# A 31-tap depthwise convolution: 28 instead of 25 taps of each second chunk on TensorE, as three products of split operands, with the diagonals built by GpSimd

## Chip, core and metric

The kernel runs on one core of a Trainium2 chip. The metric is the device time of one execution in microseconds (us). Engines are named as in the profile: PE is TensorE (PEld its weight loads), DVE VectorE, ACT ScalarE, POOL GpSimd, SP SyncE, which here only issues DMAs.

## What is computed

A stack of two blocks over 256 tokens of width 1024, all in float32. The change is in one layer of the second block, a convolution module between a feed-forward layer and a cross attention:

```python
def conformer_conv(x, norm, w1, b1, dw_w, dw_b, ln_g, ln_b, w2, b2):
    h = rms_norm_2(x, norm) @ w1 + b1
    h = jax.nn.glu(h, axis=-1)
    h = causal_dwconv(h, dw_w, dw_b)
    h = jax.nn.silu(layer_norm_2(h, ln_g, ln_b))
    return h @ w2 + b2
```

`causal_dwconv` has 31 taps: each of the 1024 features is summed over itself and its 30 predecessors in time, each with a weight of its own per feature. The rest of the stack (attention forms, recurrences, pooling, feed-forward layers) is the same in both kernels.

## The kernel before

Features stand on the 128 partitions and the 256 tokens along the free dimension, so the 1024 features of the convolution are eight chunks of 128 x 256. Every weight matrix comes from DRAM in pieces of 128x1024 (`raw`); ACT rounds a piece to `wh`, DVE subtracts to get the rest, `wl` (L289 and L290, the helper `weights`), and each product is three matmuls of 256 columns: high by high, high by low, low by high (L302, the helper `mm_F`, results `psF`).

The function `conformer` goes over four pairs of chunks. For a pair it projects the gate and the value (`psF`), scales both out of PSUM on DVE (`c_g` L1061, `c_a` L1064), applies tanh and bias on ACT, and forms the gated value `a` (the second `c_a`, L1069). Then it convolves. `CONV_PE = (0, 25) + (0, 25) * 3` says how many taps of a chunk go to TensorE: none of the first chunk of a pair, 25 of the second. The other taps are DVE instructions that add one shifted, weighted copy to `c_h` (L1094, SCALAR_TENSOR_TENSOR): 30 for the first chunk after one TENSOR_SCALAR (L1087), 6 for the second. A tap on TensorE is a matmul of `a` with a diagonal matrix of that tap's weights, in plain float32, accumulated in one bank, `ps_conv`; the diagonals `c_diag` are 100 ACT instructions (L1081, identity times a column of weights). ACT then moves `ps_conv` with the bias to `c_h` (L1085).

After the last pair a filler follows, two projections of the next layer's memory (`kF`, whose products are `psF` too), and then the layer norm over features: `c_acc` (L1099, L1101) sums the chunks on DVE, `ps_mean` (L1104) sums partitions on PE.

A scheduler orders the instructions of each engine before the run; on the chip each engine works through its list in that order, and an instruction that waits holds up those behind it. Tiles of one tag share a fixed number of buffers: tag `f4` has 9, used in this layer by `c_h` (two tiles, the second from the third pair on) and by `c_diag`; a new tile waits until the readers of an old one are done. On POOL the kernel before has only small work: the power in the reciprocal rms (`x_rc`, L111), masks, memsets. The `x_rc` of this layer stands right before the first pair.

Of the kernel before, what the change touches and what calls it, by code (L numbers as in the profile page):

```python
# [11 lines left out]
F32 = mybir.dt.float32  # L12
# [18 lines left out]
def shape_constants():  # L31
    """Tables that depend on shapes alone."""
    t = np.arange(S, dtype=np.float64)
    gamma = 1.0 - 2.0 ** (-5.0 - np.arange(NH, dtype=np.float64))
    dec = np.zeros((128, 3, NH, 128), np.float64)
    for b, (s0, t0) in enumerate(((0, 0), (0, 128), (128, 128))):
        s, q = t[s0:s0 + 128, None], t[None, t0:t0 + 128]
        seen = (s // CHUNK) <= (q // CHUNK)
        for h in range(NH):
            dec[:, b, h] = np.where(seen, gamma[h] ** np.abs(q - s), 0.0) * 128.0 ** -0.5  # L40
    misc = np.zeros((128, 32), np.float64)
    misc[:, 0] = 10000.0 ** (-(np.arange(128) % 64) / 64.0)
    misc[:, 1] = np.where(np.arange(128) < 64, 1.0, -1.0)
    misc[:, 16:32] = 1.0 / np.arange(1, 17)
    return dec.reshape(128, -1).astype(np.float32), misc.astype(np.float32)


CONV_PE = (0, 25) + (0, 25) * 3
KV_AHEAD = 400
# [4 lines left out]
def stack_kernel(ctx: ExitStack, tc: tile.TileContext, I: dict, out: bass.AP):  # L54
# [16 lines left out]
    def t_f4(shape, name):  # L71
        return f4.tile(shape, F32, tag="f4", name=name)
# [18 lines left out]
    def bc(ap, n):  # L91
        """[128, m] -> [128, n, m]"""
        return ap.unsqueeze(1).to_broadcast([ap.shape[0], n, ap.shape[1]])

    # ---------------------------------------------------------------- constants
    ident = const.tile([128, 128], F32, name="ident")
# [15 lines left out]

    # ---------------------------------------------------------------- activations in
    def load_T(src, name):
        """[256, 1024] -> four pairs [128 features, 2 chunks, 256 tokens]"""
        raws = []
        for t in range(2):
            raw = wraw.tile([128, D], F32, tag="wraw", name=name + "_raw")
            nc.sync.dma_start(raw, src[t * 128:(t + 1) * 128, :])
            raws.append(raw)  # L120
        return raws
# [3 lines left out]

    # ---------------------------------------------------------------- parameters as columns
    order = ["norm_pre", "norm_post", "mem_norm", "conv_q", "conv_k",
# [43 lines left out]

    # ---------------------------------------------------------------- helpers
    def sums_to_rstd(acc, name):
        """acc [128, 256]: partial sums of squares -> column [128, 2] of 1 / rms"""
        ps = bank([128, 2], "ps_ss")
        for t in range(2):
            PE.matmul(ps[:, t:t + 1], acc[:, t * 128:(t + 1) * 128], ones[:, 0:1], start=(t == 0),
                      stop=True, skip_group_check=True)
        rc = t_sm([128, 2], name + "_rc")
        V.tensor_scalar(rc, ps, 1.0 / D, EPS, op0=ALU.mult, op1=ALU.add)  # L180
        rsqrt(rc, rc)
        return rc

    def row_of(rc, name):
        """column [128, 2] -> [128, 256], the same on each partition"""
        pb = bank([128, S], "ps_rb")
# [7 lines left out]
    def softplus_neg_abs(dst, src):  # L194
        """log(1 + exp(-|src|)), small tiles: 2 atanh(e / (2 + e)) as a series"""
        sh = [128, int(np.prod(src.shape[1:]))]
# [15 lines left out]
    class Sq:  # L212
        """sum of squares of four pairs of chunks, by partition"""

# [23 lines left out]
    class Operand:  # L238
        """float32 [128, n, 256] as two float32r parts whose sum it is"""

# [15 lines left out]
    class Norm:  # L256
        """what a layer reads of x: x times the gain as an operand, and the reciprocal rms"""

# [18 lines left out]
    def weights(src, n_k):  # L277
        """[n_k * 128, n] of DRAM -> slices (hi, lo) by chunk"""
        parts = []
# [14 lines left out]
    def mm_F(pss, src, op, k0, n_k, first, last):  # L294
        """features on partitions: banks of two chunks from the columns of src"""
        w = weights(src, n_k)
# [9 lines left out]
    def mm_T(pss, src, op, k0, n_k, first, last, extra=None):  # L306
        """tokens on partitions: two banks of 128 tokens by 512 columns"""
        w = weights(src, n_k)
# [27 lines left out]
    def scaled_F(pss, rb, dst):  # L336
        """dst [128, 4, 256] = psum * rstd"""
        for i in range(2):
            V.tensor_tensor(dst[:, 2 * i:2 * i + 2], pss[i], bc(rb, 2), op=ALU.mult)
# [17 lines left out]
    def silu2_F(w, c0, op, rb, name, pss=None):  # L357
        """2 * silu(projection), features on partitions"""
        z = F_plain(w, c0, op, rb, name, pss=pss)
# [5 lines left out]
    def silu2_T(w, c0, op, rc, name):  # L365
        """2 * silu(projection) / rstd, tokens on partitions"""
        pss = proj_T(w, c0, op)
# [8 lines left out]
    def taps(dst, src, wname, j0, stride, n_tap, first):  # L376
        """dst = causal convolution of src [128, 256] along time, per-feature taps"""
        tap = lambda j: col(wname, j0 + j * stride)
# [11 lines left out]
    def blocks(kF, qF, fn):  # L390
        """products of keys (partitions) and queries, by block of 128 x 128"""
        for b, (s, t) in enumerate(BLK):
# [10 lines left out]
    def T_to_operand(y, scale):  # L403
        """[128 tokens, 2, 512] -> operand of 4 chunks"""
        o = Operand(4, yop, "y")
# [10 lines left out]

    # ---------------------------------------------------------------- memory
    def mem_stats(src):
# [23 lines left out]

    # ---------------------------------------------------------------- rotary tables
    cosF = const.tile([128, S], F32, name="cosF")
# [28 lines left out]

    # ================================================================ block 1
    def layer(l, nrm, early, kv, late, nxt):
# [7 lines left out]
        rb = row[0]  # L483
        # small parameters
        bif = t_sm([128, 2, 4], "bif")
# [19 lines left out]

        # ---- stick breaking
        def sb_branch():
# [56 lines left out]

        # ---- mLSTM
        def conv_silu2(c0, wname, name):
            """2 * silu(causal convolution of a projection), features on partitions"""
            x = F_plain(w, c0, op, rb, name + "_x")
# [8 lines left out]
        def ml_branch():  # L577
            # gates: tokens on partitions, then rows
            ps = t_sm([128, 2, 8], "gsum")
# [111 lines left out]

        # ---- retention
        def rt_branch():
# [50 lines left out]

        # ---- gated mixing over tokens
        def gm_branch():
# [51 lines left out]

        # ---- attention to the memory
        def xa_branch():  # L800
# [25 lines left out]

        # ---- gated merge
        merged = [t_f4([128, 2, 512], "merged")
# [46 lines left out]
    def softmax(pairs, sc):  # L875
        """softmax over keys of sum of q^T k, queries on partitions: [128, 2, 256]"""
        pl = bank([128, 2, S], "ps_lg")
# [26 lines left out]

    # ================================================================ block 2
    def kv_k(op, rb, w, c0):
# [44 lines left out]
    def mixer_ab(nrm, fill_1, fill_2, nxt):  # L951
# [6 lines left out]
        rb = row[0]  # L958
        # ---- gated linear recurrence
        wgx = t_f4([128, 8, 128], "a_gx")  # L960
# [4 lines left out]
        for g4 in range(2):  # L965
# [15 lines left out]
            th = t_f4([128, 4, S], "a_th")  # L981
            # q = 1 - exp(la) = -tanh(la / 2) (1 + exp(la)); the squared multiplier is q (2 - q)
            A.activation(th, la, AF.Tanh, scale=-0.5)
# [11 lines left out]
        for g4 in range(2):  # L995
# [5 lines left out]
            for i in range(2):  # L1001
                ya.put(slice(2 * i, 2 * i + 2), z[:, 2 * i:2 * i + 2])
        # ---- pooling over several windows
        pss = proj_F(w, 2 * D, op)
# [44 lines left out]
    def conformer(nrm, fill_1, fill_2, nxt):  # L1049
# [8 lines left out]
        for i in range(4):  # L1058
# [12 lines left out]
            for m in range(2):  # L1071
# [3 lines left out]
                if n_pe:  # L1075
                    ps = bank([128, S], "ps_conv")
                    for j0 in range(0, n_pe, 8):
                        n = min(8, n_pe - j0)
                        dg = t_f4([128, 8, 128], "c_diag")
                        for j in range(j0, j0 + n):  # L1080
                            A.activation(dg[:, j - j0], ident, AF.Copy,  # L1081
                                         scale=col("c_dw_w_2", (30 - j) * 8 + c))
                            PE.matmul(ps[:, j:], dg[:, j - j0], a[:, m, 0:S - j], start=(j == 0),  # L1083
                                      stop=(j == n_pe - 1))
                    A.activation(h, ps, AF.Identity, bias=col("c_dw_b_2", c))  # L1085
# [130 lines left out]
    class Last:  # L1216
        """x times the last gain, in place, and the sums of squares of x"""

# [20 lines left out]

    # ================================================================ program  # L1240
    nrm = Norm("norm_pre", 0)
# [99 lines left out]
```

## Time and profile before

| | |
|---|---|
| median of 3 runs | 1837.79 us (1835.53 to 1839.57) |
| span of the profiled execution | 1834.2 us |
| stretch of the four pairs | about 1394 to 1496 us of the span |

The span is the time from the first to the last instruction of the one profiled execution. It lies 3.6 us under the median of the timed runs; that difference holds what is around the span and the scatter between executions. All positions below are microseconds from the start of the span. Busy time of PE is modelled: matmuls overlap, so the pace of TensorE is read from starts, not from durations.

### The profile page before, as it was taken

What the parts mean: (1) busy time and instruction counts of PE and PEld (TensorE: products, weight loads), DVE (VectorE), ACT (ScalarE), POOL (GpSimd) and SP (SyncE); (2) the same over time, 40 slices, a digit from 0 to 9 for tenths busy, and PEclk for the clock granted to TensorE, in tenths of its full rate; (3) what the DMA queues carried; (4) which work ended last, traced back from release to release, by engine and by line L of the source; (5) the groups of instructions that cost most, each with busy time, mean ns of one, the idle gap of its engine ahead of it and who ended that gap; (6) DMA issues with size and microseconds to landing.
All of it is one profiled execution on the core that took longest, in us unless ns stands there. A gap on an engine that the chain in (4) does not pass through costs nothing.

```text
span 1834.2 us, 30422 instructions
## 1 busy us (share of the span) xinstructions
PE 1788.3 (97%) x12246; PEld 1665.9 (91%) x12246; DVE 1264.4 (69%) x1883; ACT 963.0 (53%) x1372; POOL 40.2 (2%) x52
## 2 busy tenths in 40 slices
PE   7999999999999999999999899999999989999998
PEld 7988988888999899888899798999999989899998
DVE  5796855666657877666667965576669985477665
ACT  4764345454555543555456854455447545455444
POOL 0100000000000000000000000000000000000000
PEclk9999999999999999999999999999999999999999
DMA  6456455666554655567655454455554344355552
GB/s 212 150 179 197 153 183 157 195 208 193 161 161 145 201 166 165 153 196 230 193 186 161 146 177 144 141 182 184 184 184 143 104 134 150 113 175 186 183 184 92
DMA packets 168002, 309.56 MB, mean 169 GB/s; under 512 B 12620, under 2 KB 25268, under 8 KB 167860
## 3 DMA queue, kind: packets, MB, share of 16 engines
q1 hardware_dynamic: 166480, 307.08, 53.8%
q8 instruction: 96, 1.57, 0.4%
q10 hardware_dynamic: 1380, 0.53, 0.1%
q14 instruction: 46, 0.38, 0.1%
HBM read 306.52 MB, written 1.05 MB: 168 GB/s over the span
## 4 chain that ended last, share of the span: by engine, by line
PE 75%; issue 15%; DVE 5%; ACT 3%; DMA 1%; POOL 0%; SPq 0%; POOLq 0%; ACTq 0%; DVEq 0%
PE psF L302 35%; PE psT L315 19%; PE psO L302 14%; DVE c_h L1094 2%; DVE wl L290 1%; PE ps_conv L1083 1%; PE ps_lg L880 1%; PE ps_blk L395 1%; ACT wh L289 1%; PE ps_xo L1162 1%; DMA gm_wr<-in_gm_ws 1%; PE ps_rb L188 0%; PE ps_rt L724 0%; PE ps_num L650 0%; DMA raw<-in_w_in 0%
## 5 line engine op out<-in xcount | busy, mean ns | idle before, releaser
L290 DVE TENSOR_TENSOR wl<-raw,wh 128x1024 fp32r<-128x1024 f32 x560 | 670.6, 1222 | 337.7 <-ACT wh L289 330.3
L289 ACT ACTIVATE wh<-raw 128x1024 fp32r<-128x1024 f32 x560 | 574.9, 1055 | 515.8 <-PE psF L302 174.2
L302 PE MATMUL psF<-xh,wh 128*128 128x256 f32 x1888 | 539.6, 286 | 8.3 <-ACT wh L289 5.3
L302 PE MATMUL psF<-xh,wl 128*128 128x256 f32 x1888 | 536.2, 285 | 2.3 <-DVE wl L290 2.3
L302 PE MATMUL psF<-xl,wh 128*128 128x256 f32 x1888 | 536.7, 285 | 0.0
L302 PEld LDWEIGHTS psF<-xh,wh 128*128 128x128 f32 x1888 | 364.4, 193 | 10.2 <-ACT wh L289 6.1
L302 PEld LDWEIGHTS psF<-xh,wl 128*128 128x128 f32 x1888 | 364.0, 193 | 3.5 <-DVE wl L290 3.1
L302 PEld LDWEIGHTS psF<-xl,wh 128*128 128x128 f32 x1888 | 364.5, 193 | 0.6
L302 PE MATMUL psO<-yh,wh 128*128 128x256 f32 x800 | 225.7, 285 | 5.4 <-ACT yh L247 5.4
L302 PE MATMUL psO<-yl,wh 128*128 128x256 f32 x800 | 227.4, 285 | 0.5 <-DVE yl L248 0.5
L302 PE MATMUL psO<-yh,wl 128*128 128x256 f32 x800 | 226.1, 283 | 0.0
L315 PE MATMUL psT<-wh,xl 128*128 128x512 f32 x544 | 216.0, 397 | 0.0
L315 PE MATMUL psT<-wl,xh 128*128 128x512 f32 x544 | 215.4, 396 | 0.0
L315 PE MATMUL psT<-wh,xh 128*128 128x512 f32 x544 | 213.4, 392 | 0.0
L302 PEld LDWEIGHTS psO<-yh,wh 128*128 128x128 f32 x800 | 153.5, 193 | 6.4 <-ACT yh L247 6.4
L302 PEld LDWEIGHTS psO<-yl,wh 128*128 128x128 f32 x800 | 153.9, 193 | 0.9 <-DVE yl L248 0.7
L302 PEld LDWEIGHTS psO<-yh,wl 128*128 128x128 f32 x800 | 154.0, 193 | 0.1
L315 PEld LDWEIGHTS psT<-wl,xh 128*128 128x128 f32 x544 | 102.2, 188 | 21.0
L315 PEld LDWEIGHTS psT<-wh,xl 128*128 128x128 f32 x544 | 102.2, 188 | 20.6
L315 PEld LDWEIGHTS psT<-wh,xh 128*128 128x128 f32 x544 | 102.3, 188 | 19.2
L1094 DVE SCALAR_TENSOR_TENSOR c_h<-c_a,cols,c_h 128x229 f32<-128x229 f32 (+15 forms) x144 | 63.2, 464 | 3.0
L315 PE MATMUL psT<-wl,yh 128*128 128x512 f32 x160 | 62.3, 389 | 0.0
(379 smaller groups left out, 2115.4 us busy)
## 6 DMA issues: line engine op xcount, KB each, us to landing
raw<-in_w_in SPq DMA_DIRECT2D x224, 512.0 KB, 3.9
raw<-in_f_w_up SPq DMA_DIRECT2D x96, 512.0 KB, 4.7
raw<-in_f_w_down SPq DMA_DIRECT2D x48, 512.0 KB, 4.7
raw<-in_w_up SPq DMA_DIRECT2D x40, 512.0 KB, 3.5
raw<-in_c_w_pw SPq DMA_DIRECT2D x24, 512.0 KB, 4.4
raw<-in_ab_w_in SPq DMA_DIRECT2D x20, 512.0 KB, 3.7
raw<-in_w_mem_kv SPq DMA_DIRECT2D x16, 512.0 KB, 4.9
raw<-in_w_out SPq DMA_DIRECT2D x16, 512.0 KB, 3.8
```

Of the source, the lines that this page charges most:

```text
L289: A.activation(hi, raw, AF.Copy)
L290: V.tensor_tensor(lo, raw, hi.bitcast(F32), op=ALU.subtract)
L302: PE.matmul(pss[m // 2][:, m % 2], a, b, start=(first and m % 2 == 0 and k == 0 and n == 0), stop=(last and k == n_k - 1 and n == 2), skip ...
L315: PE.matmul(pss[t], a, b, start=(first and k == 0 and n == 0), stop=(last and k == n_k - 1 and n == 2), skip_group_check=True)
L395: PE.matmul(ps[:, h], kF[:, h, s * 128:s * 128 + 128], qF[:, h, t * 128:t * 128 + 128], start=(h == 0), stop=True, skip_group_check=True)
L880: PE.matmul(pl[:, t], q[:, t * 128:t * 128 + 128], k, start=(t == 0 and n == 0), stop=(n == len(pairs) - 1), skip_group_check=True)
L1083: PE.matmul(ps[:, j:], dg[:, j - j0], a[:, m, 0:S - j], start=(j == 0), stop=(j == n_pe - 1))
L1094: V.scalar_tensor_tensor(h[:, j:], a[:, m, 0:S - j], col("c_dw_w_2", (30 - j) * 8 + c), h[:, j:], op0=ALU.mult, op1=ALU.add)
L1162: PE.matmul(po[:, dj], vT[i][:, m, c0:c0 + 128], pT[:, m], start=(dj == 0 and m == 0), stop=(m == 1), skip_group_check=True)
```

## The change

Only the convolution's TensorE part changes (and docstrings and comments are gone, which moves line numbers).

- `CONV_PE` is 28 for each second chunk: DVE keeps 3 of its taps instead of 6.
- The moving operand is no longer `a` in float32 but `c_hl`: two rounded (float32r) parts whose sum is `a`, each behind 32 zeros. POOL writes the zeros, ACT the high part, DVE the low part (L1081 of the new file).
- The tap weights are split likewise: `c_wt`, two small DVE instructions per pair (CAST and TENSOR_TENSOR of 128x31). It has one buffer.
- The diagonals are built by POOL, four taps with both parts at a time: a TENSOR_TENSOR of 128x1024 that multiplies a broadcast of `c_wt` by a broadcast of the identity, seven per pair (L1092). ACT builds none.
- Each tap is three matmuls of 256 columns (L1098) in place of one float32 matmul.
- `c_hl` and all `c_diag` take buffers of tag `f4`.

```diff
 
 
-CONV_PE = (0, 25) + (0, 25) * 3
+CONV_PE = (0, 28) + (0, 28) * 3
+PAD = 32
 KV_AHEAD = 400
 AHEAD = {"start": 60, "layer": 100, "ab": 100, "xa": 100, "ffn": 100, "conf": 100}
...
@@ -1074,14 +1075,29 @@
                 n_pe = CONV_PE[c]
                 if n_pe:
                     ps = bank([128, S], "ps_conv")
-                    for j0 in range(0, n_pe, 8):
-                        n = min(8, n_pe - j0)
-                        dg = t_f4([128, 8, 128], "c_diag")
+                    hl = f4.tile([128, 2, PAD + S], F32R, tag="f4", name="c_hl")
+                    G.memset(hl[:, :, 0:PAD].bitcast(F32), 0.0)
+                    A.activation(hl[:, 0, PAD:], a[:, m], AF.Copy)
+                    V.tensor_tensor(hl[:, 1, PAD:], a[:, m], hl[:, 0, PAD:].bitcast(F32),
+                                    op=ALU.subtract)
+                    wt = sm.tile([128, 31, 2], F32R, tag="c_wt", name="c_wt", bufs=1)
+                    b0 = base["c_dw_w_2"] + c
+                    raw = cols[:, b0:b0 + 241:8]
+                    V.tensor_copy(wt[:, :, 0], raw)
+                    V.tensor_tensor(wt[:, :, 1], raw, wt[:, :, 0].bitcast(F32), op=ALU.subtract)
+                    for j0 in range(0, n_pe, 4):
+                        n = min(4, n_pe - j0)
+                        dg = f4.tile([128, 4, 2, 128], F32R, tag="f4", name="c_diag")
+                        some = wt[:, 31 - j0 - n:31 - j0].bitcast(F32)
+                        G.tensor_tensor(dg[:, 0:n], some.unsqueeze(3).to_broadcast([128, n, 2, 128]),
+                                        ident.unsqueeze(1).unsqueeze(1)
+                                        .to_broadcast([128, n, 2, 128]), op=ALU.mult)
                         for j in range(j0, j0 + n):
-                            A.activation(dg[:, j - j0], ident, AF.Copy,
-                                         scale=col("c_dw_w_2", (30 - j) * 8 + c))
-                            PE.matmul(ps[:, j:], dg[:, j - j0], a[:, m, 0:S - j], start=(j == 0),
-                                      stop=(j == n_pe - 1))
+                            d = dg[:, n - 1 - (j - j0)]
+                            for i, (x, y) in enumerate(((0, 0), (0, 1), (1, 0))):
+                                PE.matmul(ps, d[:, x], hl[:, y, PAD - j:PAD - j + S],
+                                          start=(j == 0 and i == 0),
+                                          stop=(j == n_pe - 1 and i == 2))
                     A.activation(h, ps, AF.Identity, bias=col("c_dw_b_2", c))
                 else:
                     V.tensor_scalar(h, a[:, m], col("c_dw_w_2", 240 + c), col("c_dw_b_2", c),
```

The lists of three engines show the move. On POOL, the rows around this layer, before:

```order
L111 TENSOR_TENSOR post_rc<-post_rc,nhalf 128x2
L111 TENSOR_TENSOR x_rc<-x_rc,nhalf 128x2 x4
L111 TENSOR_TENSOR cln_rc<-cln_rc,nhalf 128x2
L111 TENSOR_TENSOR x_rc<-x_rc,nhalf 128x2 x3
L1328 UNCONDITIONAL_BRANCH
```

and in the changed kernel:

```order
L112 TENSOR_TENSOR x_rc<-x_rc,nhalf 128x2 x4
L1079 MEMSET c_hl 128x2x32
L1092 TENSOR_TENSOR c_diag<-c_wt,ident 128x1024 x7
L1079 MEMSET c_hl 128x2x32
L1092 TENSOR_TENSOR c_diag<-c_wt,ident 128x1024 x7
L1079 MEMSET c_hl 128x2x32
L1092 TENSOR_TENSOR c_diag<-c_wt,ident 128x1024 x7
L1079 MEMSET c_hl 128x2x32
L1092 TENSOR_TENSOR c_diag<-c_wt,ident 128x1024 x7
L112 TENSOR_TENSOR cln_rc<-cln_rc,nhalf 128x2
```

All 28 diagonal instructions stand behind the fourth `x_rc`, the one of this layer.

On DVE, the first pair of chunks from the gate on, before:

```order
L1061 TENSOR_TENSOR c_g<-psF,x_rb 128x512
L1064 TENSOR_TENSOR c_a<-psF,x_rb 128x512
L290 TENSOR_TENSOR wl<-raw,wh 128x1024
L1069 SCALAR_TENSOR_TENSOR c_a<-c_g,c_a 128x512
L1087 TENSOR_SCALAR c_h<-c_a,cols 128x256
L1094 SCALAR_TENSOR_TENSOR c_h<-c_a,cols,c_h 128x255
L290 TENSOR_TENSOR wl<-raw,wh 128x1024
L1094 SCALAR_TENSOR_TENSOR c_h<-c_a,cols,c_h 128x254
```

and now:

```order
L1062 TENSOR_TENSOR c_g<-psF,x_rb 128x512
L1065 TENSOR_TENSOR c_a<-psF,x_rb 128x512
L291 TENSOR_TENSOR wl<-raw,wh 128x1024
L1070 SCALAR_TENSOR_TENSOR c_a<-c_g,c_a 128x512
L1103 TENSOR_SCALAR c_h<-c_a,cols 128x256
L1110 SCALAR_TENSOR_TENSOR c_h<-c_a,cols,c_h 128x255
L291 TENSOR_TENSOR wl<-raw,wh 128x1024
L1081 TENSOR_TENSOR c_hl<-c_a,c_hl 128x256
L1110 SCALAR_TENSOR_TENSOR c_h<-c_a,cols,c_h 128x254
```

The matmuls of the convolution could start after `c_a` (L1069); now they wait for `c_hl`, which stands four instructions later. In the fourth pair it stands three later. The `c_wt` of the second pair follows nine taps behind the first `c_hl`, that of the third pair right behind the second pair's `c_a`, that of the fourth pair ten taps behind the third `c_hl`; the first pair's is done long before, in the first block.

On PE, around the fourth pair's convolution as it stands now (`psF` are the filler's products, `mh` and `ml` the memory's two parts):

```order
L303 MATMUL psF<-mh,wl 128x256
L1098 MATMUL ps_conv<-c_hl,c_diag 128x256
L303 MATMUL psF<-mh,wh 128x256
L303 MATMUL psF<-ml,wh 128x256
L303 MATMUL psF<-mh,wl 128x256
L303 MATMUL psF<-mh,wh 128x256
L1098 MATMUL ps_conv<-c_hl,c_diag 128x256 x83
L303 MATMUL psF<-ml,wh 128x256
L303 MATMUL psF<-mh,wl 128x256
```

One matmul of the convolution now stands ahead of four of the filler, and the other 83 behind them. Before, the 25 stood together, with 99 `psF` matmuls between the third convolution and the fourth and 143 between the fourth and `ps_mean`; now these counts are 83 and, with the four, 159.

## Rows read from the trace of the kernel before

**Rows 1.** The page: busy time, share of the span and instructions of each engine.

```profile
PE 1788.3 (97%) x12246; PEld 1665.9 (91%) x12246; DVE 1264.4 (69%) x1883; ACT 963.0 (53%) x1372; POOL 40.2 (2%) x52
```

**Rows 2.** Busy time by stretch: start:end, length, each engine, granted clock, DMA.

```profile
core 0: us, PE busy (x) PEld busy (x) DVE busy (x) ACT busy (x) POOL busy (x), PEclk, DMA share, GB/s
1399.00:1420.00 21.00, 20.35 (x134) 19.36 (x134) 20.26 (x42) 19.73 (x58) 0.00 (x0) 1.00 0.17 56
1420.00:1443.00 23.00, 23.00 (x156) 22.21 (x157) 22.29 (x44) 6.29 (x10) 0.00 (x0) 1.00 0.34 102
1443.00:1466.00 23.00, 23.00 (x159) 22.20 (x158) 22.19 (x45) 19.48 (x57) 0.00 (x0) 1.00 0.35 111
...
1514.00:1518.00 4.00, 3.45 (x15) 3.29 (x16) 1.85 (x3) 4.00 (x8) 0.00 (x0) 0.57 0.36 126
```

**Rows 3.** The chain that ended last, 1380 to 1600: start us, length us.

```profile
1391.53 1.35 POOL x_rc L111
...
1400.47 0.49 DVE c_h L1094
1400.99 0.49 DVE c_h L1094
...
1468.35 10.56 PE ps_conv L1083 x50
1478.91 17.14 PE psF L302 x143
1496.05 0.86 PE ps_mean L1104 x4
```

**Rows 4.** TensorE in order of time: start us, length us, line, names, count.

```profile
1398.85 10.56 PE L1083 MATMUL ps_conv<-c_a,c_diag 128*128 128x256 f32 x50
1409.07 0.45 PE L302 MATMUL psF<-xh,wh 128*128 128x256 f32 x1
```

**Rows 5.** VectorE in order of time, from 1394 us to 1468 us.

```profile
1394.09 0.69 DVE L1061 TENSOR_TENSOR c_g<-psF,x_rb 128x512 f32<-128x512 f32 x1 [1.77 <-ACT x_rb L191]
...
1395.65 1.22 DVE L290 TENSOR_TENSOR wl<-raw,wh 128x1024 fp32r<-128x1024 f32 x1 [0.27 <-ACT wh L289]
1397.25 0.69 DVE L1069 SCALAR_TENSOR_TENSOR c_a<-c_g,c_a 128x512 f32<-128x512 f32 x1 [0.37 <-ACT c_a L1068]
1397.98 0.41 DVE L1087 TENSOR_SCALAR c_h<-c_a,cols 128x256 f32<-128x256 f32 x1
...
1398.83 1.22 DVE L290 TENSOR_TENSOR wl<-raw,wh 128x1024 fp32r<-128x1024 f32 x1
...
1432.64 4.52 DVE L1094 SCALAR_TENSOR_TENSOR c_h<-c_a,cols,c_h 128x231 f32<-128x231 f32 x12
...
1467.61 0.68 DVE L1069 SCALAR_TENSOR_TENSOR c_a<-c_g,c_a 128x512 f32<-128x512 f32 x1
```

**Rows 6.** TensorE waits, 1390 to 1500: us in total, times, longest.

```profile
PE ps_conv L1083 <- DVE c_a L1069: 2.0, 2, 1.4
```

**Rows 7.** All engines in order of time, around 98 us.

```profile
98.15 1.23 POOL L625 TENSOR_SCALAR_AFFINE_SELECT ml_d<-ml_d 128x512 f32<-128x512 f32 x2 [19.79 <-ACT ml_d L620]
...
98.77 1.28 DVE L385 SCALAR_TENSOR_TENSOR mlq<-mlq_x,cols,mlq 128x253 f32<-128x253 f32 x2 [1.98 <-ACT mlq L380]
```

**Rows 8.** One line, 90 to 105 us: duration ns min/median/max, starts, forms.

```profile
L385 DVE SCALAR_TENSOR_TENSOR mlq<-mlq_x,cols,mlq x12: 469/475/884, 94.3 to 101.1; 128x253 f32<-128x253 f32 x4, 128x254 f32<-128x254 f32 x4, 128x255 f32<-128x255 f32 x4
```

**Rows 9.** All engines in order of time, around 62 us.

```profile
61.83 0.64 POOL L521 TENSOR_SCALAR_AFFINE_SELECT sb_abs<-sb_abs 128x512 f32<-128x512 f32 x1 [13.26 <-DVE sb_abs L519]
...
62.01 1.52 DVE L290 TENSOR_TENSOR wl<-raw,wh 128x1024 fp32r<-128x1024 f32 x1 [0.26 <-ACT wh L289]
```

**Rows 10.** Groups of GpSimd instructions: busy us, mean ns, idle before.

```profile
L111 POOL TENSOR_TENSOR post_rc<-post_rc,nhalf 128x2 f32<-128x2 f32 x2 | 1.4, 697 | 362.7 <-DVE post_rc L180 362.7
```

**Rows 11.** All engines in order of time, around 983 us.

```profile
983.44 2.36 DVE L290 TENSOR_TENSOR wl<-raw,wh 128x1024 fp32r<-128x1024 f32 x2
...
983.60 1.62 POOL L111 TENSOR_TENSOR x_rc<-x_rc,nhalf 128x2 f32<-128x2 f32 x1 [31.97 <-DVE x_rc L180]
```

## Prediction

> **What bounds the kernel now.** I read the page first, then the stretches of the convolution, then the chain that ended last, then the two engines it names in order of time. The page says that PE is busy for 97% of the span and POOL for 2% [rows 1]: whole-kernel shares, which hide what this layer looks like. The stretches do not: in the three pairs of chunks from 1399 to 1466 us DVE is busy 20.26 of 21, 22.29 of 23 and 22.19 of 23 us, PE just as fully, and POOL does nothing at all [rows 2]. So two engines are full side by side, and whichever gets more work sets the pace. The chain passes through the taps on DVE, which follow each other at 0.515 us when each waits for the one before (starts 1400.47 and 1400.99), then through the fourth convolution at 1468.35, then through 143 `psF` matmuls in 17.14 us to `ps_mean` at 1496.05 [rows 3]. PE waits for the gated value `c_a` twice, 2.0 us in all [rows 6]: that is the slack of PE against DVE.
>
> **What the change does to each engine, if they did not meet.** PE: the 25 float32 matmuls of a chunk run from 1398.85 to the next `psF` at 1409.07, so 10.22 us [rows 4]. The 84 new ones have the shape and operand kinds of `psF`, whose pace is 17.14 / 143 = 0.120 us [rows 3]: 10.08 us. That is 0.14 us less per chunk, practically nothing: three more taps for the same time.
>
> ACT loses 100 diagonals. It was never what PE waited for in this layer (the only waits for data are those 2.0 us for DVE), so I put that at nothing; what covered it is DVE and PE being full. Its new copies into `c_hl` cost nothing either: they run while DVE does the instructions that stand ahead of its own `c_hl`. If DVE were quicker there, a copy could be late by no more than the 0.41 us of a DVE instruction over as many columns [rows 5].
>
> DVE, up to the fourth pair's `c_a` (three pairs): nine taps fewer at 0.37 us, the pace of interleaved taps (twelve in 4.52 us [rows 5]), so -3.3; their nine partners now stand alone and pay 0.515 instead of 0.37, +1.3; three `c_hl` at most at the 0.41 us of the TENSOR_SCALAR of as many columns, +1.2; six small `c_wt` instructions, between nothing and 0.41 each, I take 0.2, +1.2. Together +0.4.
>
> **Where they meet.** POOL gets 28 instructions that each read two operands of 1024 elements per partition, while DVE streams instructions that also read two operands from SBUF. The trace has few such meetings, but they agree. At 98 us POOL runs two masks over 512 elements, 1.23 us together, one alone taking 0.64, so the second begins at 98.15 + 0.59 = 98.74. DVE issues a tap at 98.77 [rows 7]. That tap takes 884 ns where its kind takes 475 [rows 8]: it stood still for 0.41 us, until 99.18, which is 0.44 us after the mask began. At 62 us a mask begins at 61.83 and a `wl` at 62.01 takes 1.52 us [rows 9] instead of 1.22 [rows 5]: held until 62.31, 0.48 us after the mask's start. So POOL's reading of 512 elements stops a two-operand DVE instruction for 0.44 to 0.48 us. The other way round, the power `x_rc` takes 0.70 us alone [rows 10], but 1.62 when it comes just after a `wl` has begun; it still ends before the second of two back-to-back `wl` does [rows 11]. So POOL waits for the running DVE instruction and then gets its turn before the next one: the two alternate, one for one, and neither starves.
>
> [...]
>
> **The price of one hold.** A `c_diag` reads 1024 elements twice. Per 512 elements 0.44 to 0.48, so 1.76 to 1.92 us for four times that; I take 1.85. From below: if the broadcast operand costs no reading, one operand, 0.88 to 0.96. From above: the mask's whole pitch of 0.59 per 512, 2.36.
>
> [...]
>
> **The sum, pair by pair.** POOL is behind its `x_rc`, which ends at 1391.53 + 1.35 = 1392.88 [rows 3]; the first `c_diag` reads from about 1393.0 to 1394.85. DVE then waits for data or scales `c_g` and `c_a` out of PSUM (1394.09 on [rows 5]), so this one is free. The second begins 0.15 later (0.59 less 0.44) and ends at 1396.85; `wl`, ready at 1395.65, comes 1.2 late, of which 0.37 us of idle before `c_a` at 1397.25 takes back a part: +0.8. The other five come one after each of `wl`, `c_a`, TENSOR_SCALAR, the first tap and `wl`, all ahead of `c_hl`: 5 x 1.85 = 9.25. First pair: **+10**. PE's first matmul of the convolution waits there, with all `psF` behind it.
>
> The second pair's seven diagonals can start when `c_wt` is written, nine taps later, and when buffers come free from the running convolution, one per 1.44 us (12 matmuls); at 1.85 plus a tap each, POOL is through long before the second `c_a`. So all seven hold DVE inside the first pair. Of the third pair's, six fit into the second pair (with both `c_h` there are seven `f4` buffers, one of them `c_hl`), the seventh falls into the third, with six of the fourth pair's. 7 + 6 + 7 = 20 holds before the fourth `c_a`: **+37**. Some of them run while DVE scales `c_g` and `c_a` out of PSUM, 1.2 us per pair: no row shows whether those are held; I take them as not held, and POOL active for over half the time: **-2** (0 at the other end). With DVE's own +0.4 the fourth `c_a` is 45.4 us late.
>
> Behind it: the convolution started 0.1 us after `c_a` (1467.61 and 0.68 [rows 5], 1468.35 [rows 3]); now a tap, a TENSOR_SCALAR and `c_hl` come first, +1.2. Then PE has 159 `psF` matmuls instead of 143 to do before `ps_mean`, less 0.14 for the convolution: +1.8. And PE will have stood idle for over ten microseconds ahead of it. [...] The last diagonal's hold is covered by those `psF` matmuls, as DVE's tail was before.
>
> Sum: 10 + 37 - 2 + 0.4 + 1.2 + 1.8 + 1.7 = **+50 us**. The profiled span of 1834.2 becomes 1884.3; the median of the runs lay 3.6 above that span, so **1888 us**, 2.7% slower.
>
> **Rivals.**
> *Half the hold.* If only one operand's reading stops DVE (0.93): the first pair costs 0.1 + 4 x 0.93 = 3.8, the twenty 18.6, less 1, plus the same 5.1: +26.5, **1864 us**. For it: one operand repeats 128 times, the other is one small matrix. Against: the rows know only one-operand masks, so nothing shows that a broadcast is read for less.
> *POOL becomes the bound.* If a `c_diag` takes much longer than it reads, say 4 us, seven are 28 us per pair, over the 23.5 us that a pair takes now (1397.25 to 1467.61 for three [rows 5]). For it: the power on POOL takes 0.70 us for two elements [rows 10], so its arithmetic can be slow; against: the masks run at 0.59 us per 512. With no hold at all it would cost 13 us in the first pair (PE's last diagonal at 1393 + 28 + 1.44 instead of an end at 1409.07) and three times 4.5 after: +27. With a hold as long it would be 27 x 3.8: about +100, **1937 us**. It decides from 23.5 / 7 = 3.4 us per diagonal on.
> *Not slower.* If DVE is not stopped (POOL's reads of these patterns are short, or give way), seven diagonals at 2 us fit into a pair, and what is left is DVE's +0.4, `c_hl`'s +1.2, PE's +1.8, less up to 2.0 of PE's waits for `c_a` and whatever ACT's relief gives its neighbours: -2 to +3.4 us, **1836 to 1841 us**. It needs 27 holds worth no more than a few tenths of a microsecond in all; at 0.1 us each it is already lost. Against it stand the stretched tap, the stretched `wl` and the waiting `x_rc` [rows 7 to 11]; for it only that no row has this very instruction.
>
> **How the numbers follow.** Full holds 0.62, half holds 0.14, not stopped 0.13, POOL as the bound 0.11. The full hold between its bounds gives 1885 (1.76) to 1902 (2.36). The range has to leave out no more than 2 in 10: down to a little under the half hold at its lower bound (0.88, 1863), up to where a slow POOL begins to set the pace, 1858 to 1915; what is left out is the not-stopped case and about half of the slow POOL. A measurement here tells 0.2% (3.7 us) from no change; of the not-stopped case a part is within that and a part, with all of PE's waits recovered, beyond it: faster 0.04, same 0.09, slower 0.87.
>
> **What the profile after would show.** If right: POOL's 28 `c_diag` alternate with DVE taps, and taps beside them take 2.2 to 2.4 us instead of 0.47, while taps away from them are as before; the first convolution starts near 1410; pairs follow each other at over 30 us; PE's waits for `c_hl` grow to tens of microseconds with dips of the granted clock behind them; `ps_mean` comes near 1546. If the taps keep 0.47 us throughout, the hold is wrong and with it the sum; if DVE is stretched by about 0.9 us per diagonal, the second operand is; if DVE and PE both wait for POOL, the third rival holds.

## The result and the profile after

The changed kernel takes 1878.66 us, median of 4 runs (1876.6 to 1881.44), beside 1838.59 us (1835.53 to 1839.57, 4 runs) of the kernel before on the same chip: the ratio is 1.022, 95% interval 1.0205 to 1.0234. The profiled span is 1876.3 us, 42.1 us more than before.

The busy line of the page after, beside [rows 1]:

```profile
PE 1801.9 (96%) x12382; PEld 1681.0 (90%) x12382; DVE 1303.3 (69%) x1883; ACT 935.8 (50%) x1276; POOL 98.5 (5%) x84
```

The whole-kernel shares hardly move: PE falls from 97 to 96%, POOL rises from 2 to 5%. The windows over the pairs show it, beside [rows 2]:

```profile
1399.00:1420.00 21.00, 12.61 (x93) 12.24 (x92) 20.55 (x21) 2.46 (x3) 15.56 (x9) 0.84 0.16 51
1420.00:1443.00 23.00, 14.72 (x107) 14.26 (x106) 22.71 (x31) 5.55 (x9) 9.83 (x5) 0.80 0.21 64
1443.00:1466.00 23.00, 21.73 (x166) 21.52 (x164) 22.22 (x30) 2.48 (x3) 12.17 (x7) 0.90 0.09 29
```

DVE is as full as before but gets through 21 instructions in the first stretch instead of 42. PE, full before, is busy for 12.61 of 21 us, and its granted clock is 0.84 where it was 1.00 (within the stretch 1.00 up to 1406 us, 0.50 from 1407 to 1413 and 1.00 from 1414 on). What stretches DVE is seen with POOL beside it. POOL in order of time (start us, length us):

```profile
1393.08 1.29 POOL L112 TENSOR_TENSOR x_rc<-x_rc,nhalf 128x2 f32<-128x2 f32 x1 [206.94 <-DVE x_rc L181]
...
1394.43 15.68 POOL L1092 TENSOR_TENSOR c_diag<-c_wt,ident 128x1024 fp32r<-128x1024 f32 x7
...
1415.71 14.12 POOL L1092 TENSOR_TENSOR c_diag<-c_wt,ident 128x1024 fp32r<-128x1024 f32 x7 [2.27 <-DVE c_wt L1087]
...
1449.93 12.02 POOL L1092 TENSOR_TENSOR c_diag<-c_wt,ident 128x1024 fp32r<-128x1024 f32 x6 [1.29 <-PE ps_conv L1098]
1477.28 1.96 POOL L1092 TENSOR_TENSOR c_diag<-c_wt,ident 128x1024 fp32r<-128x1024 f32 x1 [15.32 <-PE ps_conv L1098]
...
1481.85 12.10 POOL L1092 TENSOR_TENSOR c_diag<-c_wt,ident 128x1024 fp32r<-128x1024 f32 x6 [2.50 <-DVE c_wt L1087]
```

And DVE in the first of these bursts, beside [rows 5]:

```profile
1395.60 0.69 DVE L1062 TENSOR_TENSOR c_g<-psF,x_rb 128x512 f32<-128x512 f32 x1 [1.77 <-ACT x_rb L192]
1396.20 0.68 DVE L1065 TENSOR_TENSOR c_a<-psF,x_rb 128x512 f32<-128x512 f32 x1
1397.15 2.12 DVE L291 TENSOR_TENSOR wl<-raw,wh 128x1024 fp32r<-128x1024 f32 x1 [0.27 <-ACT wh L290]
1399.19 2.38 DVE L1070 SCALAR_TENSOR_TENSOR c_a<-c_g,c_a 128x512 f32<-128x512 f32 x1
1401.62 1.87 DVE L1103 TENSOR_SCALAR c_h<-c_a,cols 128x256 f32<-128x256 f32 x1
1403.52 2.00 DVE L1110 SCALAR_TENSOR_TENSOR c_h<-c_a,cols,c_h 128x255 f32<-128x255 f32 x1
1405.44 2.91 DVE L291 TENSOR_TENSOR wl<-raw,wh 128x1024 fp32r<-128x1024 f32 x1
1408.28 2.11 DVE L1081 TENSOR_TENSOR c_hl<-c_a,c_hl 128x256 fp32r<-128x256 f32 x1
...
1440.28 0.68 DVE L1070 SCALAR_TENSOR_TENSOR c_a<-c_g,c_a 128x512 f32<-128x512 f32 x1
...
1504.53 0.68 DVE L1070 SCALAR_TENSOR_TENSOR c_a<-c_g,c_a 128x512 f32<-128x512 f32 x1
...
1506.55 0.68 DVE L1115 TENSOR_TENSOR c_acc<-c_h 128x512 f32<-128x512 f32 x1
```

Seven `c_diag` stand in 15.68 us. The first meets no DVE instruction that it stops, the second holds a `wl` for 0.9 us (2.12 instead of 1.22), and from the third on each has one DVE instruction beside it that takes 1.5 to 1.7 us longer than its kind: `c_a` 2.38 instead of 0.69, TENSOR_SCALAR 1.87 instead of 0.41, `wl` 2.91 instead of 1.22. The two that read PSUM (`c_g`, `c_a` at 1395.60 and 1396.20) are not stretched at all: 0.69 and 0.68 us, as before ([rows 5] for `c_g`; `c_a` here):

```profile
1394.70 0.68 DVE L1064 TENSOR_TENSOR c_a<-psF,x_rb 128x512 f32<-128x512 f32 x1
```

The chain that ended last (start us, length us) goes through the same taps, beside [rows 3]:

```profile
1413.40 0.49 DVE c_h L1110
1413.91 0.49 DVE c_h L1110
...
1415.96 2.00 DVE c_h L1110
1417.98 2.00 DVE c_h L1110
...
1507.28 10.64 PE ps_conv L1098 x83
1517.92 18.60 PE psF L303 x155
1536.52 0.86 PE ps_mean L1120 x4
```

Taps away from a diagonal keep their pitch (1413.40 to 1413.91, 0.51 us); taps beside one follow each other at about 2.02 us (1415.96 to 1417.98). One diagonal costs DVE 2.02 - 0.515 = **1.51 us**. PE's waits show where that goes (1385 to 1560 us: us in total, times, longest), beside [rows 6]:

```profile
PE psF L303 <- DVE wl L291: 14.2, 3, 5.6
PE ps_conv L1098 <- ACT c_hl L1080: 7.3, 3, 3.0
PE ps_conv L1098 <- DVE c_hl L1081: 7.0, 2, 6.8
```

Waits of 2.0 us in all for DVE have become 28.5, all behind DVE or behind what DVE held up (ACT's copy into `c_hl` waits for DVE's `c_a`, 3.5 us in three waits): POOL's diagonals themselves are not among the things that PE waits for.

### The profile page after: what moved, and what is told of

It reads as the page before. It is cut to its first block, busy times and chain, and to the rows that moved or that the text cites. A ratio compares the mean times of both kernels' runs of the same rounds, so it can differ in the third digit from the quotient of the medians.

```text
span 1876.3 us, 30668 instructions
## 1 busy us (share of the span) xinstructions
PE 1801.9 (96%) x12382; PEld 1681.0 (90%) x12382; DVE 1303.3 (69%) x1883; ACT 935.8 (50%) x1276; POOL 98.5 (5%) x84
## 3 DMA queue, kind: packets, MB, share of 16 engines
q10 hardware_dynamic: 1380, 0.53, 0.1%
## 4 chain that ended last, share of the span: by engine, by line
PE 73%; issue 15%; DVE 7%; ACT 3%; DMA 1%; POOL 0%; SPq 0%; ACTq 0%; DVEq 0%; POOLq 0%
PE psF L303 34%; PE psT L316 19%; PE psO L303 14%; DVE c_h L1110 4%; DVE wl L291 1%; PE ps_lg L881 1%; PE ps_blk L396 1%; PE ps_xo L1178 1%; ACT wh L290 1%; DMA gm_wr<-in_gm_ws 1%; PE ps_conv L1098 1%; PE ps_rb L189 0%; PE ps_rt L725 0%; PE ps_num L651 0%; DMA raw<-in_w_in 0%
## 5 line engine op out<-in xcount | busy, mean ns | idle before, releaser
L303 PE MATMUL psF<-xh,wl 128*128 128x256 f32 x1888 | 538.0, 286 | 11.4 <-DVE wl L291 11.3
L1110 DVE SCALAR_TENSOR_TENSOR c_h<-c_a,cols,c_h 128x228 f32<-128x228 f32 (+12 forms) x132 | 93.3, 719 | 3.0
L1098 PE MATMUL ps_conv<-c_hl,c_diag 128*128 128x256 f32 x336 | 47.3, 305 | 15.9 <-ACT c_hl L1080 7.3
```

Source lines behind the costliest of these rows:

```text
L303: PE.matmul(pss[m // 2][:, m % 2], a, b, start=(first and m % 2 == 0 and k == 0 and n == 0), stop=(last and k == n_k - 1 and n == 2), skip ...
L1098: PE.matmul(ps, d[:, x], hl[:, y, PAD - j:PAD - j + S], start=(j == 0 and i == 0), stop=(j == n_pe - 1 and i == 2))
L1110: V.scalar_tensor_tensor(h[:, j:], a[:, m, 0:S - j], col("c_dw_w_2", (30 - j) * 8 + c), h[:, j:], op0=ALU.mult, op1=ALU.add)
```

## Experiments

Three theories. **T1**: the time is lost because POOL's reading of its operands stops DVE; it is the number of diagonals before the fourth `c_a` times the stop. **T2**: it is lost in the convolution's own new parts, in the three products, the split input that PE waits for, and the new order. **T3**: POOL stops DVE, but at a price per instruction, whatever it reads. The times, each against the kernel before on the same chip (1838.1 to 1838.9 us), and the distance between one gated value (L1069 or its like) and the next, from the starts of these instructions on DVE, for the three pairs:

| kernel | median us | ratio, 95% interval | pair 1, 2, 3 (us) |
|---|---|---|---|
| before | 1838.59 | | 22.00, 23.90, 24.46 |
| changed | 1878.66 | 1.0220 (1.0205 to 1.0234) | 41.09, 31.61, 32.64 |
| e1_two | 1894.45 | 1.0305 (1.0289 to 1.0320) | 36.62, 37.79, 36.93 |
| e2_one | 1858.13 | 1.0102 (1.0085 to 1.0118) | 27.54, 28.73, 27.92 |
| e3_none | 1838.40 | 1.0001 (0.9991 to 1.0010) | 22.60, 23.89, 24.45 |
| e6_select | 1859.46 | 1.0115 (1.0100 to 1.0130) | 31.56, 27.56, 27.05 |
| e4_dve | 1863.19 | 1.0128 (1.0110 to 1.0146) | 22.24, 24.70, 33.30 |
| e5_act | 1841.86 | 1.0015 (1.0006 to 1.0024) | 20.08, 29.40, 22.89 |
| e7_act25 | 1839.02 | 1.0003 (0.9993 to 1.0013) | 20.26, 26.00, 22.33 |
| e8_pool25 | 1858.03 | 1.0103 (1.0087 to 1.0119) | 33.31, 28.75, 22.54 |
| e9_half | 1871.12 | 1.0178 (1.0161 to 1.0195) | 39.06, 30.90, 30.94 |

The rows of DVE before that this table and the sections below add to [rows 5]:

```profile
1419.25 0.69 DVE L1069 SCALAR_TENSOR_TENSOR c_a<-c_g,c_a 128x512 f32<-128x512 f32 x1
1443.15 0.68 DVE L1069 SCALAR_TENSOR_TENSOR c_a<-c_g,c_a 128x512 f32<-128x512 f32 x1
1466.29 0.68 DVE L1099 TENSOR_TENSOR c_acc<-c_h 128x512 f32<-128x512 f32 x1
...
1490.61 0.69 DVE L1101 TENSOR_TENSOR c_acc<-c_acc,c_h 128x512 f32<-128x512 f32 x1
```

**POOL work that nobody needs, added to the kernel before (e1, e2, e3).** The convolution stays as it was; behind each gated value stand seven POOL instructions on one spare `f4` buffer.

```diff
+            un = t_f4([128, 8, 128], "c_un")
+            for k in range(7):
+                G.tensor_tensor(un, a[:, 1, 0:128].unsqueeze(1).to_broadcast([128, 8, 128]),
+                                ident.unsqueeze(1).to_broadcast([128, 8, 128]), op=ALU.mult)
             chains = []
```

In e2 the instruction is `G.affine_select(un, a[:, 1, 0:128]...)`, with one operand; in e3 it is `G.memset(un, 0.0)`.

> The kernel before, with 28 TENSOR_TENSOR of 128x1024 added on GpSimd (seven for each of the four pairs of diagonals, two operands read, results unused; nothing is left out). Theory T1 (GpSimd's reading of its operands stops VectorE, so that each VectorE instruction beside one costs about 1.5 us more): the 21 instructions that stand before the fourth c_a cost 21 x 1.5 = 32 us, and the last seven some 6 us more, so 1870 to 1880 us, and taps beside them at 2.0 us. Theory T2 (the loss of the change comes from its own new waits, TensorE for the second plane of the diagonals or for c_hl, and from the three products): nobody waits for the added instructions, so 1838 us, no change.

> The kernel before, with 28 affine_select of 128x1024 added on GpSimd at the same places (one operand read instead of two; results unused, nothing left out). T1 (time goes by the elements that GpSimd reads): half the hold, about 0.75 us each, so 21 x 0.75 = 16 us and a little behind it: 1853 to 1860 us. T3 (time goes by the instruction, whatever it reads): as with two operands, 1870 to 1880 us. T2: 1838 us.

> The kernel before, with 28 memsets of 128x1024 added on GpSimd at the same places (no operand read; results unused, nothing left out). T1 and T2: 1838 us, no change, taps beside them at 0.49 us. If GpSimd's writes stopped VectorE too: up to 20 us more.

The chain of e1, taps beside POOL:

```profile
1408.68 2.52 DVE c_h L1098
1411.22 2.54 DVE c_h L1098
```

The chain of e2, the same place:

```profile
1405.49 1.20 DVE c_h L1099
1406.72 1.20 DVE c_h L1099
```

And POOL and DVE of e3 in order of time:

```profile
1395.09 5.03 POOL L1072 MEMSET c_un<- 128x1024 f32 x5
...
1398.22 1.00 DVE L1090 TENSOR_SCALAR c_h<-c_a,cols 128x256 f32<-128x256 f32 x1
...
1405.94 7.48 DVE L1097 SCALAR_TENSOR_TENSOR c_h<-c_a,cols,c_h 128x244 f32<-128x244 f32 x16
1406.12 7.02 POOL L1072 MEMSET c_un<- 128x1024 f32 x7 [6.01 <-PE ps_conv L1086]
```

T2 is not needed for a loss: with the old convolution untouched, added POOL reading alone costs 56 us (e1). Whether T2 adds to it is for e5 to say. T3 falls: one operand costs 20 us where two cost 56, and none costs nothing; sixteen taps beside seven memsets take 7.48 us, 0.47 each. (A memset waits for no operand, so those of e3 ran earlier than the instructions of e1 (the first at 1280.9 us, in e1 at 1397.8), seven of the 28 even before the layer; the rest ran beside taps.) The length of the POOL instruction alone is not the price either: a memset takes 1.01 us (5.03 / 5) and stops no tap, while an `affine_select` takes 1.1 (e6) and stops one for 0.7.

But e1 missed its number on the high side. Its pitch is 2.5 us, a stop of 1.99 instead of 1.51, and seven of these are the 12.5 to 14.6 us by which each pair is longer. It reads as many elements as a `c_diag`, so elements alone do not set the price. The pattern differs (runs of 128 elements, eight times over, where `c_diag` reads each element 128 times); that this is the cause was not tested. The three pairs make 41 of the 56 us. The other 15 came behind the fourth `c_a`, where the fourth pair's seven stops put off the `wl` of the filler, for which PE then waits up to 9.7 us:

```profile
PE psF L302 <- DVE wl L290: 24.5, 4, 9.7
```

In e2 the pitch is 1.23 us and a stop 0.71.

**One operand in the changed kernel (e6).** Every other instruction stands where it stood.

```diff
-                        G.tensor_tensor(dg[:, 0:n], some.unsqueeze(3).to_broadcast([128, n, 2, 128]),
-                                        ident.unsqueeze(1).unsqueeze(1)
-                                        .to_broadcast([128, n, 2, 128]), op=ALU.mult)
+                        G.affine_select(dg[:, 0:n], some.unsqueeze(3).to_broadcast([128, n, 2, 128]),
+                                        pattern=[[0, n], [0, 2], [-1, 128]],
+                                        compare_op=ALU.is_equal, fill=0.0, base=0,
+                                        channel_multiplier=1)
```

> The changed kernel, with each pair of diagonals made by an affine_select that reads c_wt alone (one operand read instead of two); every other instruction stands where it stood. T1: the hold falls from 1.51 us to about half, and the 25 or so VectorE instructions that are held before the fourth c_a give back some 19 us: 1855 to 1863 us. T3 (time goes by the instruction): no change from the changed kernel, 1875 to 1882 us. T2 (the loss is the new waits of TensorE): no change either, 1875 to 1882 us, unless the select itself is much shorter.

The chain of e6, taps beside the fourth pair's diagonals:

```profile
1469.29 1.20 DVE c_h L1111
1470.51 1.21 DVE c_h L1111
```

Again a stop of about 0.71 us, and half of the loss is back, as T1 has it. Nothing of T2 was touched. In the bursts before, where a tap and a diagonal begin within 0.03 us of each other (1414.52 and 1414.55), the next tap is 1.43 us off, a stop of 0.92: the loss seems to depend on how far POOL's instruction has come when the tap starts.

**Another engine builds the diagonals (e4, e5, e7).** In e4 the multiplication is `V.tensor_tensor`. In e5 it is two ScalarE activations per tap; e7 is e5 with 25 taps.

```diff
-                        G.tensor_tensor(dg[:, 0:n], some.unsqueeze(3).to_broadcast([128, n, 2, 128]),
-                                        ident.unsqueeze(1).unsqueeze(1)
-                                        .to_broadcast([128, n, 2, 128]), op=ALU.mult)
+                        for q in range(n):
+                            for x in range(2):
+                                A.activation(dg[:, q, x], ident, AF.Copy, scale=some[:, q, x:x + 1])
```

> The changed kernel, with the diagonals built by VectorE itself instead of GpSimd; nothing else is changed. T1: VectorE then does each 128x1024 product itself, for about 1.1 us by its cost for a product of that size, and is never held; 28 x 1.1 = 31 us of its own in place of some 25 holds of 1.5 us (38 us): about 1868 us, still far from before. T2 (the loss is TensorE's new waits and the three products): about the changed kernel's 1878 us.

> The changed kernel, with the diagonals built by ScalarE (two 128x128 activations for each diagonal, 14 for each seven) instead of GpSimd; 28 taps stay on TensorE with three products. T1: nothing holds VectorE, so the time falls back to 1836 to 1846 us (ScalarE's own load of some 22 us per pair of rows could make it a few us more). T2 (the loss is in the three products and their waits): it stays at 1870 to 1880 us.

> The kernel with ScalarE building the diagonals and 25 taps on TensorE in each second chunk, in three products. T1: nothing holds VectorE, three taps more on it, TensorE with three taps (1.2 us per chunk) less: 1834 to 1844 us. T2: as with 28 taps on ScalarE's diagonals, 1870 to 1880 us.

The chain of e4 goes through the diagonals on DVE:

```profile
1399.84 6.81 DVE c_diag L1092 x6
```

and PE now has one long wait, behind DVE's last sum:

```profile
PE ps_mean L1120 <- DVE c_acc L1117: 10.9, 1, 10.9
```

DVE does the whole multiplication itself and the kernel is 15 us faster than with POOL doing it beside DVE: a `c_diag` takes 6.81 / 6 = 1.13 us of DVE's chain when DVE builds it, 1.51 when POOL does. It came out 5 us lower than expected. An estimate: the diagonals add 28 x 1.13 = 31.6 us to DVE, but before, the last `c_acc` ended at 1490.61 + 0.69 = 1491.30 and `ps_mean` started at 1496.05 [rows 3]: 4.75 us of that is slack, and 26.9 is left, beside a span that is 26.5 us longer (1860.7 us). That the two agree so well is in part luck, because DVE's list up to the last `c_acc` also has twelve taps fewer and seven `wl` more, which the estimate leaves out.

With ScalarE nothing is held and the time is back to within 3 us, with 28 taps in three products on TensorE. So those are not where the loss was, and they bring nothing either. A window of e5 shows what the engines do then:

```profile
1466.00:1490.00 24.00, 24.00 (x202) 24.00 (x202) 23.19 (x44) 23.98 (x67) 0.00 (x0) 1.00 0.36 115
```

DVE has fewer taps, but now ScalarE is full (23.98 of 24 us), and so is PE, as it was. With 25 taps (e7) it cannot be told from the kernel before. No run beat that kernel.

**One part of the change alone (e8).** The kernel before, 25 plain taps; only its diagonals are built by GpSimd, eight taps at a time.

```diff
                         dg = t_f4([128, 8, 128], "c_diag")
+                        b1 = base["c_dw_w_2"] + c + 8 * (31 - j0 - n)
+                        G.tensor_tensor(dg[:, 0:n], cols[:, b1:b1 + 8 * n - 7:8].unsqueeze(2)
+                                        .to_broadcast([128, n, 128]),
+                                        ident.unsqueeze(1).to_broadcast([128, n, 128]), op=ALU.mult)
                         for j in range(j0, j0 + n):
-                            A.activation(dg[:, j - j0], ident, AF.Copy,
-                                         scale=col("c_dw_w_2", (30 - j) * 8 + c))
...
```

> One part of the change alone: the kernel before, with its 25 taps, one product each and 4-byte input as it was, but with each conv's 25 diagonals built by GpSimd in three TENSOR_TENSOR of 128x1024 and one of 128x128 instead of 25 ScalarE activations. T1 (a hold of 1.5 us for 2048 elements read): three whole holds and a small one per conv, 4.7 us, three convs before the fourth c_a: 14 us, and up to 5 for the fourth, so 1852 to 1858 us. T3 (per instruction): four holds per conv, 18 us and up to 6: 1856 to 1862 us. T2 (the loss is the split and its three products): 1838 us.

POOL and DVE of e8 at the start of the layer:

```profile
1392.34 3.79 POOL L1081 TENSOR_TENSOR c_diag<-cols,ident 128x1024 f32<-128x1024 f32 x2
...
1393.59 0.69 DVE L1061 TENSOR_TENSOR c_g<-psF,x_rb 128x512 f32<-128x512 f32 x1 [1.77 <-ACT x_rb L191]
1394.20 0.68 DVE L1064 TENSOR_TENSOR c_a<-psF,x_rb 128x512 f32<-128x512 f32 x1
...
1481.74 0.69 DVE L1069 SCALAR_TENSOR_TENSOR c_a<-c_g,c_a 128x512 f32<-128x512 f32 x1
```

the main wait of its PE in the layer:

```profile
PE ps_conv L1085 <- DVE c_a L1069: 16.5, 4, 11.1
```

and the chain behind the fourth `c_a`:

```profile
1482.58 12.22 PE ps_conv L1085 x50
1494.80 19.19 PE psF L302 x160
```

This one part costs 19 us, with no split anywhere: T2 is out here too. The time lies at the top of T1's range and inside T3's, so it does not tell those two apart. The fourth `c_a` is 14.1 us late (1481.74 instead of 1467.61). That is the 14 us expected of three convolutions' holds, but by luck: all twelve whole diagonals, the fourth convolution's too, had run by 1447.70, and the pairs are 11.3, 4.9 and -1.9 us longer. Most of the rest came behind it: the fourth convolution takes 12.22 us instead of 10.56, and 160 `psF` matmuls instead of 143 follow it, 19.19 us instead of 17.14 [rows 3]. No gain from the relief of ScalarE, which this part brings as the change does, is to be seen. The rows show one thing more: two diagonals beside DVE instructions that read PSUM stand in 3.79 us, a pitch of 1.90, and neither side is stretched.

**Twice as many POOL instructions of half the size (e9).**

```diff
-                        G.tensor_tensor(dg[:, 0:n], some.unsqueeze(3).to_broadcast([128, n, 2, 128]),
-                                        ident.unsqueeze(1).unsqueeze(1)
-                                        .to_broadcast([128, n, 2, 128]), op=ALU.mult)
+                        for q in range(0, n, 2):
+                            G.tensor_tensor(dg[:, q:q + 2], some[:, q:q + 2].unsqueeze(3)
+                                            .to_broadcast([128, 2, 2, 128]),
+                                            ident.unsqueeze(1).unsqueeze(1)
+                                            .to_broadcast([128, 2, 2, 128]), op=ALU.mult)
```

> The changed kernel, with each pair of diagonal planes built by twice as many GpSimd instructions of half the size (two of 128x512 in place of one of 128x1024). T1 (time goes by the elements read): twice the holds, half as long each (about 0.75 us, so a tap beside one at 1.2 to 1.3 us), and the same sum: 1874 to 1884 us. T3 (a hold has a price per instruction, whatever its size): twice the holds of 1.5 us, 1905 to 1920 us. A hold with a fixed part in it would come out between.

The chain of e9, and POOL with a PSUM reader of DVE in order of time:

```profile
1412.78 1.15 DVE c_h L1112
1413.95 1.14 DVE c_h L1112
```

```profile
1419.45 6.99 POOL L1093 TENSOR_TENSOR c_diag<-c_wt,ident 128x512 fp32r<-128x512 f32 x6
...
1423.15 0.68 DVE L1062 TENSOR_TENSOR c_g<-psF,x_rb 128x512 f32<-128x512 f32 x1
```

A pitch of 1.17, a stop of about 0.65: twice that is 1.30, less than the 1.51 of one whole instruction. T3, which wanted 1905 to 1920, falls again; 1871 us lies just under T1's range, so splitting gave back some 7 us, of which the stops explain at most 28 x 0.21 = 6. `c_g`, which reads PSUM, takes its 0.68 in the middle of POOL's burst.

## Why the prediction was right

The mechanism is the one forecast, and 1878.66 lies in the range, 9 us under the 1888. The range is wide: e6, with half the stop, lies in it too, so it is the pitch of the taps and not the time that tells the full hold from the half. Term by term, the shift of the fourth `c_a` first: it starts 36.9 us later (1504.53 against 1467.61 on [rows 5]). Of that 1.55 us is there before the layer begins (`x_rc` starts at 1393.08 after, 1391.53 on [rows 3]); such a difference is in other kernels too (1391.20 in e1, 1393.16 in e2). So 35.4 us are the change's, where the sum had 45.4.

- *The price of one hold*, 1.85, is the step that was mis-sized: it measured 1.51. The count was right: seven, six and seven holds in the three pairs (the bursts of 7, 6, 1 and 6 on POOL, the first seven apart), and in the first pair five whole ones and a part. At 1.51 the twenty cost 30.2 instead of 37, and the first pair 8.4 instead of 10: `wl` 0.9 late, with 0.5 of it taken back by the idle time, then 1.69, 1.46, 1.51, 1.69 and 1.69 for the five (each row above less its kind: [rows 5], 0.49 us for the tap, 0.42 for `c_hl`). The step that failed was to charge DVE from the start of POOL's instruction. In the rows behind the price DVE lost 0.41 us (884 less 475 ns) and 0.30 (1.52 less 1.22); the forecast took 0.44 and 0.48, counted from the mask's start, and multiplied these by four. Counted so, the price is about right: the first diagonal of the second burst begins at 1415.71, the tap beside it at 1415.96, and held for 1.51 us this tap is free at 1417.47, which is 1.76 after the diagonal's start. But DVE pays only from its own start on.
- *The credit of 2 us* for holds that fall on DVE's reading of PSUM: its premise is shown, its amount is not. `c_g` and `c_a` took 0.69 and 0.68 beside POOL, in the changed kernel, in e8 and in e9. But in the later pairs of the changed kernel the burst ended before `c_g` came (1415.71 + 14.12 = 1429.83, `c_g` started at 1432.01), so no hold was saved there.
- *DVE's own work*, +0.4, came out as 35.4 - 8.4 - 30.2 = -3.2. About half of that is order, which the forecast left out: two `c_acc` instructions of 0.68 us, which stood ahead of the fourth `c_a` before (the first at 1466.29), now stand behind it (1506.55), and so does one tap. Another part is `c_wt`, put at 1.2: a `c_wt` instruction between two taps that wait for each other costs nothing (taps at 1414.43, 1414.94 and 1415.45 keep their 0.51 us with one between each two). The rest was not taken apart. That this and the missing credit of 2 us work against each other is luck.
- *Behind the fourth `c_a`*: 4.7 forecast (`c_hl`, PE's longer tail, the clock), 5.2 measured (42.1 of the span less 36.9). Up to `ps_mean` it is 3.6 (1536.52 against 1496.05, less 36.9), where all 4.7 stood; the other 1.6 came after it and was not taken apart. The clock term, 1.7 us, is shown by no run at this place; an estimate of the same size follows from the mean of 0.57 over 4 us on [rows 2], 4 x 0.43 = 1.7 us lost there. Here it was too large: PE's waits for `c_hl` are 6.8 us at most, not over ten, and the longest of those behind ACT 3.0. The granted clock was 0.68 from 1504 to 1508 us and 0.89 from 1508 to 1512; the 83 matmuls of the fourth convolution took 10.64 us where 0.120 each would be 9.96, and the four `psF` ahead of them 0.85 where it would be 0.48: 1.1 us, not 1.7. In the pairs before, the granted clock fell to 0.80 to 0.90 as well, but there DVE set the pace.

Of the signs named beforehand, the alternation one for one, pairs of over 30 us and dips of the clock are there. Others came out smaller: a tap beside a diagonal takes 2.0 us instead of 2.2 to 2.4, PE's waits for `c_hl` are 14.3 us and not tens of microseconds (as much again, 14.2, went to `wl`, which the forecast did not name), and `ps_mean` comes at 1536.5 instead of near 1546. Of the rivals, *not slower* fell with the result, *half the hold* with the pitch of 2.02 (e2 and e6 are what it would have looked like), *POOL as the bound* because PE waited for no diagonal and a `c_diag` takes 1.9 us, under the 3.4 from which that decides.

The runs show further which DVE instructions POOL stops and which it does not: 0.47 us per tap beside memsets (e3), PSUM readers at 0.68 and 0.69 beside a `c_diag`, and a TENSOR_SCALAR of 1.87 us that was held. The stop is shorter than the POOL instruction behind it, 1.51 us beside a pitch of 1.90 with no tap beside it (e8); some of the difference is that the diagonal begins before the tap does (0.25 us in the case above).

## What to carry to other kernels

An idle engine is free only if its work does not stop a full one: POOL was busy for 2% of the span here, and its new work cost 40 us. Before moving element-wise work to GpSimd, look at what VectorE does in that stretch: where VectorE streamed two-operand SBUF instructions back to back in this case, a GpSimd instruction that reads two SBUF operands cost VectorE most of its own length (1.5 of 1.9 us), more than VectorE needs to do the work itself (1.13 us in e4). Beside such taps, GpSimd work that only writes cost nothing (0.47 us per tap in e3), and work that reads one operand instead of two cost about half (0.7 us for each instruction, still 20 us in all in e2). Beside VectorE instructions that read PSUM even two-operand work cost nothing (they took 0.68 and 0.69 us, in the changed kernel, in e8 and in e9).

## What the runs showed of the hardware that I had not expected

- A TENSOR_SCALAR with one SBUF operand (128x256) was held too: 1.87 us instead of 0.41 beside a `c_diag`, and once 1.00 us beside a POOL memset, which held no two-operand instruction (e3).
- Two POOL instructions with two operands of 1024 elements each, but in other patterns, stop DVE for 1.51 (`c_diag`) and 1.99 us (`c_un` of e1).
- Halving a POOL instruction takes its stop from 1.51 to 0.65 us, to less than half: a part of each POOL instruction was not felt by the DVE instruction beside it. An estimate from the shortest `c_diag` of each kernel (1895 ns in the changed one, 1040 in e9): 1.90 - 1.51 and 1.04 - 0.65, 0.39 us both times.
- In the changed kernel the two engines took strict turns, whichever two-operand instruction of DVE was next: no DVE instruction lost two diagonals (the most is 1.69 us, a `wl` or `c_a`), and POOL's pitch rose only from 1.90 us with no tap beside it (e8) to 2.02 beside one (more beside the longer `wl`: the first seven take 15.68 us, 2.24 each).
